# Four forms per expert, w1/w3 in 4 KB runs, and H accumulated chunk by chunk

## The chip, the cores and the metric

The kernel runs on one core of one Trainium2 chip. The metric is device time in microseconds (us) of one execution. Three runs of the kernel before gave 1067.29, 1071.5 and 1073.5 us, a median of 1071.5. The engines are called by their short names in the profile: PE (TensorE's matmuls), PEld (its weight loads), DVE (VectorE), ACT (ScalarE), POOL (GpSimd) and SP (SyncE, which issues most DMAs). A "q" behind a name (PEq, PEldq) is that engine's sequencer: it waits, branches or reads a count while the engine itself may go on with what is queued.

## The reference, cut to what matters

One layer of a hybrid attention / gating block over 1024 tokens of width 1024, followed by a mixture of experts. The change lies in the mixture alone. Every token picks one of four groups and two of its four experts; 16 experts, 512 hidden columns each:

```python
for e in range(N_EXPERTS):                                # 16
    hid = jax.nn.silu(t @ w1[e]) * (t @ w3[e])            # (1024, 512)
    out = out + gate[:, e:e + 1] * (hid @ w2[e])          # gate is zero but for two experts of a token
x = x + g_f * out
```

All arrays are float32. w1 and w3 are (16, 1024, 512), w2 is (16, 512, 1024): 6 MB of weights for an expert.

## The kernel before, in words

Before the mixture (up to about 606 us) come the modulation, the input projection, attention, gating, the output projection and the router. The router writes, for each expert, a list of its tokens, and leaves their numbers in `cnt`. From line 1536 on, the experts run one after the other in an order written out by hand: each engine executes its instructions in the order of the code.

**Tiles.** An expert takes its tokens in tiles of up to 128. `gather` (L1332) fetches the rows of a tile from `hfD` by an indirect DMA on POOL. `x_split` (L1338) transposes them on PE, eight pieces of 128 columns, and splits each into a high part (ACT) and a low part (DVE), so that a product in full float32 is made of three matmuls (`mm3`, L85: high x high, high x low, low x high). A tile of 64 tokens or fewer can go in the half form (`half_x`, `half_h`, `half_y`): the high part in the first 64 columns of the stationary operand, the low part in the other 64, so that two matmuls do in place of three and the two halves of the result are summed afterwards (`half_sum`, an ACT copy and a DVE addition). The first tile of an expert always goes in the full form, a second or third one by its count.

**Products.** H is computed in two halves f of its columns. A half (`h_mm`, L1350) takes 256 columns of w1 and 256 of w3 side by side: 8 x 3 matmuls of 512 columns. Then comes silu on ACT, a product on DVE, and `h_T` (L1362) transposes the 128 x 256 result in two pieces and splits it again. Y (`y_mm`) is 4 x 2 x 3 = 24 matmuls. So a full tile has 72 matmuls, a half one 48. `y_out` scales by the gate and adds the rows to `out` by an indirect DMA on POOL.

**Weights.** An expert's weights come in six chunks of 1 MB (`w_chunk`, L919): chunks 0 and 1 hold w1 and w3 of the first column half, 2 and 3 of the second, 4 and 5 hold w2. Chunks 0 to 3 read rows of 256 columns, 1 KB in one run; w2's runs have 4 KB. Seven raw buffers receive them; `e_conv` (L928) splits them into high parts (ACT, L941) and low parts (DVE or POOL, L946), 12 halves of 128 x 1024 for an expert, into six slots. A slot can be refilled when the expert before has finished with the chunk of the same number. A raw buffer that is free again starts the load of the chunk seven further on, from SP.

**Control flow.** `count(e)` (L1460) reads a count into a register on every engine, and `tc.If` becomes a branch on every engine. Bodies stand in the program in the order of the code; a body that isn't taken is jumped over. An expert e > 0 has an If for its second x (L1564, with `second`, L1470, choosing the form), one for the next expert's second gather (`gather_more`, L1466) and one for its second tile (`more1`, L1528: two bodies, 76 and 52 matmuls and transposes). Between them stand the first tile's parts and the conversions, written once. Expert 0's first `h_mm` is written right behind the reading of its count, outside every If.

Of the kernel before, what the change touches and what calls it, by code (L numbers as in the profile page):

```python
# [21 lines left out]
P = 128  # L22
# [17 lines left out]
def hybrid_layer_kernel(ctx, tc, a, out):  # L40
# [878 lines left out]
    def w_chunk(e, c, r, eng):  # L919
        if c < 4:  # L920
            for i, w in enumerate(("w1", "w3")):
                eng.dma_start(r.rearrange("p (k n) -> p k n", k=4)[:, :, i * 256:(i + 1) * 256],
                                  a[w][e, (c % 2) * 512:(c % 2) * 512 + 512, (c // 2) * 256:(c // 2) * 256 + 256].rearrange("(k p) n -> p k n", p=P))
        else:
            eng.dma_start(r.rearrange("p (k n) -> p k n", k=2),
                              a["w2"][e, (c - 4) * 256:(c - 4) * 256 + 256, :].rearrange("(k p) n -> p k n", p=P))

    def e_conv(g, i, eng=None):  # L928
        if g >= CH:
            return  # L930
        e_hi(g, i)
        if eng is None:
            eng = nc.gpsimd if g == 7 or i == 1 and (g == 6 or g >= 2 * 6 and g % 6 in (0, 5)) else nc.vector
        e_lo(g, i, eng)

    def e_hi(g, i):
        sl = slice(i * 1024, (i + 1) * 1024)
        if g == 7:
            nc.vector.tensor_copy(chi[g % NS][:, sl], raw[slot_of(g)][:, sl])
        else:  # L940
            nc.scalar.activation(chi[g % NS][:, sl], raw[slot_of(g)][:, sl], AF.Copy)  # L941

    def e_lo(g, i, eng):
        sl = slice(i * 1024, (i + 1) * 1024)
# [362 lines left out]
    def wk(e, c, k):  # L1307
        g = 6 * e + c
        n = 512 if c < 4 else 1024
        return chi[g % NS][:, k * n:(k + 1) * n], clo[g % NS][:, k * n:(k + 1) * n]  # L1310
# [9 lines left out]
    def bank4(j):  # L1320
        return bank(j, pst).rearrange("p (a n) -> p a n", a=4)
# [5 lines left out]
    hA = ep.tile([P, 256], F32, name="hA")  # L1327
    hB = ep.tile([P, 256], F32, name="hB")
# [9 lines left out]
    def x_split(j):  # L1338
        xg = (sc_f, xgi, xg2)[min(j, 2)]
        hi, lo = (xTi, xT0)[min(j, 1)]  # L1340
        for q in range(2):
            tr = bank4(j)
# [7 lines left out]
    def h_mm(e, j, f, hook=None):  # L1350
        hi, lo = (xTi, xT0)[min(j, 1)]
        po = bank(j, psh)
        for k in range(KD):
            wh, wl = wk(e, 2 * f + k // 4, k % 4)
            mm3(po, hi[:, k, :], lo[:, k, :], wh, wl, k == 0, k == KD - 1)
            if hook is not None and k == hook[0]:
                hook[1]()
        h = (hA, hB)[min(j, 1)]
        nc.scalar.activation(h, po[:, 0:256], AF.Silu)
        nc.vector.tensor_tensor(h, h, po[:, 256:512], op=ALU.mult)  # L1360

    def h_T(j, f):  # L1362
        hi, lo = hTs[min(j, 1)]
        h = (hA, hB)[min(j, 1)]
        tr = bank4(j)
        for i in range(2):
            nc.tensor.transpose(tr[:, i, :], h[:, i * P:(i + 1) * P], ident)  # L1367
        sl = slice(f * 2, f * 2 + 2)
        nc.scalar.activation(hi[:, sl, :], tr[:, 0:2, :], AF.Copy)
        nc.vector.tensor_tensor(lo[:, sl, :], tr[:, 0:2, :], hi[:, sl, :].bitcast(F32), op=ALU.subtract)  # L1370

    def y_mm(e, j, k0, k1):
        hi, lo = hTs[min(j, 1)]
        if k0 == 0:
            yss[j] = [bank(1, psy) for _ in range(2)]
        for k in range(k0, k1):
            wh, wl = wk(e, 4 + k // 2, k % 2)
            for i in range(2):
                sl = slice(i * 512, (i + 1) * 512)
                mm3(yss[j][i], hi[:, k, :], lo[:, k, :], wh[:, sl], wl[:, sl], k == 0, k == 3)  # L1380

    def y_out(e, j):
# [20 lines left out]
    def half_x(j):  # L1403
        xg = (xgi, xg2)[j - 1]
        for q in range(2):
            tr = bank4(1)
            for i in range(4):
                k = q * 4 + i
                nc.tensor.transpose(tr[:, i, 0:HP], xg[0:HP, k * P:(k + 1) * P], ident[0:HP, 0:HP])
            half_split(xT0[0][:, q * 4:q * 4 + 4, :], tr)  # L1410

    def half_h(e, j, f, hook=None):
        po = bank(1, psy)
        for k in range(KD):
            wh, wl = wk(e, 2 * f + k // 4, k % 4)
            nc.tensor.matmul(po, xT0[0][:, k, :], wh, start=k == 0, stop=False)
            nc.tensor.matmul(po, xT0[0][:, k, :], wl, start=False, stop=k == KD - 1)
            if hook is not None and k == hook[0]:
                hook[1]()
        s = xg2[0:HP, f * 512:(f + 1) * 512]  # L1420
        half_sum(s, po)
        h = hB[0:HP, :]
        nc.scalar.activation(h, s[:, 0:256], AF.Silu)
        nc.vector.tensor_tensor(h, h, s[:, 256:512], op=ALU.mult)

    def half_hT(f):
        tr = bank4(1)
        for i in range(2):
            nc.tensor.transpose(tr[:, i, 0:HP], hB[0:HP, i * P:(i + 1) * P], ident[0:HP, 0:HP])
        half_split(hTs[1][0][:, f * 2:f * 2 + 2, :], tr[:, 0:2, :])  # L1430

    def half_y(e, j, k0, k1):
        hs = hTs[1][0]
        if k0 == 0:
            yss[j] = [bank(1, psy) for _ in range(2)]
        for k in range(k0, k1):
            wh, wl = wk(e, 4 + k // 2, k % 2)
            for i in range(2):
                sl = slice(i * 512, (i + 1) * 512)
                nc.tensor.matmul(yss[j][i], hs[:, k, :], wh[:, sl], start=k == 0, stop=False)  # L1440
                nc.tensor.matmul(yss[j][i], hs[:, k, :], wl[:, sl], start=False, stop=k == 3)
# [12 lines left out]
    def conv2(g):  # L1454
        for i in range(2):
            e_conv(g, i)
# [13 lines left out]
    def second(e, j, one, other):  # L1470
        with tc.If(cr[e] > P * j + HP) as c:
            one()
        with c.Else():
            other()

    def x_more(e, j):
        second(e, j, lambda: x_split(j), lambda: half_x(j))

    def full(e, j):
        h_mm(e, j, 1, (2, lambda: h_T(j, 0)))  # L1480
        y_mm(e, j, 0, 1)
        h_T(j, 1)
        y_mm(e, j, 1, 4)
        y_out(e, j)

    def half(e, j):
        half_h(e, j, 1, (6, lambda: half_hT(0)))
        half_y(e, j, 0, 2)
        half_hT(1)
        half_y(e, j, 2, 4)  # L1490
        half_out(e, j)

    def more(e, j):
        def one():
# [4 lines left out]
            h_mm(e, j, 0)  # L1499
            full(e, j)  # L1500
# [3 lines left out]
        def other():  # L1504
            half_x(j)
            half_h(e, j, 0)
            half(e, j)
# [9 lines left out]
    def more1(e):  # L1517
        def one():
            if e == E - 1:
                with tc.If(cr[e] > P * 2):  # L1520
                    gather(e, 2)
            h_mm(e, 1, 0)
            full(e, 1)

        def other():
            half_h(e, 1, 0)
            half(e, 1)
        with tc.If(cr[e] > P):  # L1528
            second(e, 1, one, other)
# [159 lines left out]
```

## Time and profile before

| | |
|---|---|
| median of three runs | 1071.5 us |
| the profiled execution's own time | 1073.15 us |
| its span, first to last instruction | 1071.3 us |
| PE busy | 1004.6 us, 94% |
| PEld busy | 816.6 us, 76% |
| DVE busy | 735.4 us, 69% |
| ACT busy | 536.3 us, 50% |
| POOL busy | 381.6 us, 36% |
| moved by DMA | 255.26 MB, 238 GB/s on average |

Matmuls are pipelined, and their ends are modelled: one of 512 columns is shown as 0.39 us long while they start 0.23 us apart. A busy PE therefore says that matmuls follow each other without a gap, not that it runs at its peak; the distance between starts is the better measure. The granted clock is shown as a share of full speed. Idle time is put down to the engine that ended it; "PEq" there means that PE's own sequencer came late.

### The profile page before, as it was taken

How to read it: one execution, taken by the hardware profiler on the slowest of the kernel's cores; microseconds unless marked ns; L12 is line 12 of the kernel's file. 1: busy time of each engine (PE TensorE's matmuls, PEld its weight loads, DVE VectorE, ACT ScalarE, POOL GpSimd, SP SyncE). 2: the span in 40 equal slices, each digit the busy share in tenths (PEclk: the TensorE clock that was granted, in tenths of full speed). 3: DMA queues.
4: the chain of work that ended last, by engine and by line, in shares of the span. 5: the costliest groups of instructions: out<-in, count | busy, mean ns of one | idle time of the engine just before them, and what ended most of it. 6: DMA issues, size and time to landing. Idle time of an engine off the chain costs nothing. (4 is left out here: it accounts for less than half of the span.)

```text
span 1071.3 us, 15841 instructions
## 1 busy us (share of the span) xinstructions
PE 1004.6 (94%) x5161; PEld 816.6 (76%) x5161; DVE 735.4 (69%) x1478; ACT 536.3 (50%) x1024; POOL 381.6 (36%) x311
## 2 busy tenths in 40 slices
PE   9999899999999999999999888999998999999992
PEld 4688787876888989988888766777776888787771
DVE  2677658874627989967776858688888654765821
ACT  4643125243527989854322437476676543554611
POOL 1130321232302565641223554435645423243510
PEclk9999999999999999999999999999999999999997
DMA  9793605876757797959342698799999996886431
GB/s 325 271 316 134 200 1 177 287 237 243 252 210 263 253 352 265 322 182 324 122 149 80 202 299 287 247 332 353 346 360 353 343 294 201 292 257 194 131 60 16
DMA packets 138118, 255.26 MB, mean 238 GB/s; under 512 B 10310, under 2 KB 86726, under 8 KB 137994
## 3 DMA queue, kind: packets, MB, share of 16 engines
q1 hardware_dynamic: 122876, 201.57, 55.7%
q0 software_dynamic: 15120, 52.19, 16.1%
q8 instruction: 60, 0.98, 0.4%
q14 instruction: 62, 0.51, 0.2%
HBM read 210.45 MB, written 43.29 MB: 237 GB/s over the span
## 5 line engine op out<-in xcount | busy, mean ns | idle before, releaser
L946 DVE TENSOR_TENSOR clo<-raw,chi 128x1024 fp32r<-128x1024 f32 x140 | 174.2, 1291 | 18.8 <-ACT chi L941 17.7
L941 ACT ACTIVATE chi<-raw 128x1024 fp32r<-128x1024 f32 x166 | 162.6, 1049 | 1.5 <-DMA raw<-in_w 1.3
L86 PE MATMUL po<-whi,hhi 128*128 128x512 f32 x352 | 146.0, 415 | 0.0
L87 PE MATMUL po<-wlo,hhi 128*128 128x512 f32 x352 | 139.6, 397 | 0.0
L88 PE MATMUL po<-whi,hlo 128*128 128x512 f32 x352 | 139.3, 396 | 0.0
L1388 POOL DMA_INDIRECT out<-xb,lt x20 | 58.0, 2899 | 152.0 <-DVE xb L1387 152.0
L86 PE MATMUL b<-chi,yhi 128*128 128x512 f32 x256 | 104.7, 409 | 7.0 <-PEq L1528 4.1
L88 PE MATMUL b<-chi,ylo 128*128 128x512 f32 x256 | 101.7, 397 | 2.0 <-DVE ylo L1348 1.6
L87 PE MATMUL b<-clo,yhi 128*128 128x512 f32 x256 | 101.3, 396 | 0.0
L83 POOL TENSOR_TENSOR ss<-ss,nhalf 128x1 f32<-128x1 f32 (+1 forms) x36 | 46.0, 1276 | 144.2 <-DVE ss L82 144.0
L946 POOL TENSOR_TENSOR clo<-raw,chi 128x1024 fp32r<-128x1024 f32 x26 | 75.2, 2899 | 52.1 <-ACT chi L941 27.8
L86 PEld LDWEIGHTS po<-whi,hhi 128*128 128x128 f32 x352 | 66.7, 189 | 16.6 <-issue 2.6
L87 PEld LDWEIGHTS po<-wlo,hhi 128*128 128x128 f32 x352 | 66.8, 190 | 16.0 <-issue 2.4
L88 PEld LDWEIGHTS po<-whi,hlo 128*128 128x128 f32 x352 | 66.7, 189 | 15.9 <-DVE hlo L218 0.3
L86 PEld LDWEIGHTS b<-chi,yhi 128*128 128x128 f32 x256 | 48.4, 189 | 23.4 <-issue 8.4
L86 PE MATMUL yb<-chi,hhi 128*128 128x512 f32 x160 | 65.7, 411 | 0.0
L88 PE MATMUL yb<-chi,hlo 128*128 128x512 f32 x160 | 62.8, 393 | 0.0
L87 PE MATMUL yb<-clo,hhi 128*128 128x512 f32 x160 | 62.6, 391 | 0.0
L88 PEld LDWEIGHTS b<-chi,ylo 128*128 128x128 f32 x256 | 48.5, 190 | 14.1 <-DVE ylo L1348 2.1
L770 DVE TENSOR_TENSOR PT<-tr,PT 128x384 fp32r<-128x384 f32 (+1 forms) x128 | 56.4, 483 | 3.3 <-ACT PT L764 3.2
L87 PEld LDWEIGHTS b<-clo,yhi 128*128 128x128 f32 x256 | 48.5, 189 | 9.6
L572 DVE CUSTOM_DVE_ANT_0 S<-S,bt 128x640 f32<-128x640 f32 x64 | 52.7, 824 | 4.2 <-DMA bt<-in_btab 3.9
(316 smaller groups left out, 2343.7 us busy)
## 6 DMA issues: line engine op xcount, KB each, us to landing
raw<-in_w SPq DMA_DIRECT2D x104, 512.0 KB, 8.2
raw<-in_w SPq DMA_DIRECT2D x27, 1024.0 KB, 9.4
wraw<-in_w_ada SPq DMA_DIRECT2D x32, 512.0 KB, 5.1
v<-vD SPq DMA_DIRECT2D x16, 768.0 KB, 6.3
bt<-in_btab SPq DMA_DIRECT2D x32, 384.0 KB, 6.8
wraw<-in_w_in SPq DMA_DIRECT2D x20, 512.0 KB, 5.4
acc<-in_w SPq DMA_DIRECT2D x18, 512.0 KB, 7.4
wada<-in_w_ada SPq DMA_DIRECT2D x16, 512.0 KB, 6.6
```

Source lines behind the costliest of these rows:

```text
L83: nc.gpsimd.tensor_tensor(r, r, nhalf[:, :n], op=ALU.pow)
L86: nc.tensor.matmul(po, xh, wh, start=first, stop=False)
L87: nc.tensor.matmul(po, xh, wl, start=False, stop=False)
L88: nc.tensor.matmul(po, xl, wh, start=False, stop=last)
L572: nc.vector.tensor_tensor_reduce(sv, sv, btl[t, h // 2][:, h % 2 * 384:h % 2 * 384 + LK], op0=ALU.add, op1=ALU.max, scale=1.0, scalar=-3e3 ...
L770: nc.vector.tensor_tensor(lo, tr, hi.bitcast(F32), op=ALU.subtract)
L941: nc.scalar.activation(chi[g % NS][:, sl], raw[slot_of(g)][:, sl], AF.Copy)
L946: eng.tensor_tensor(lo[:, sl], r[:, sl], hi[:, sl].bitcast(F32), op=ALU.subtract)
L1388: nc.gpsimd.indirect_dma_start(out=out[:, :], out_offset=bass.IndirectOffsetOnAxis(ap=lt[:, e, j, 0:1], axis=0), in_=y, in_offset=None, co ...
```

## The change

Five things change together.

1. An expert's whole body is written four times (`expert`): one full tile, one half tile, two full tiles, a full and a half tile. Two nested If pick one by the count (expert 0 has three bodies). So a first tile of 64 tokens or fewer goes in the half form too. The x of the next expert gets its form inside the body (`next_x`).
2. Chunks 0 to 3 hold 256 rows of w1 and of w3 each, all 512 columns. Partition p takes eight rows in succession, p*8 to p*8+7, and a chunk two of them: one run of 4 KB per partition and matrix. To match, x is transposed by every eighth column (`cols`, and the first gather's `x_part`).
3. With each chunk that is there, both column halves of H advance (`h_part`), so two accumulators are open at a time.
4. A half of a chunk that is converted is now one of its two rows k, a view of 2 x 512 elements with a gap, and the third chunk's second half goes to POOL too.
5. `h_T`, `next_x` and the conversions (`fill`) stand at new places in the order; all transposes use the same two PSUM buffers, with one exception.

The diff, cut to its core:

```diff
     def w_chunk(e, c, r, eng):
         if c < 4:
             for i, w in enumerate(("w1", "w3")):
-                eng.dma_start(r.rearrange("p (k n) -> p k n", k=4)[:, :, i * 256:(i + 1) * 256],
-                                  a[w][e, (c % 2) * 512:(c % 2) * 512 + 512, (c // 2) * 256:(c // 2) * 256 + 256].rearrange("(k p) n -> p k n", p=P))
+                eng.dma_start(r[:, i * 1024:(i + 1) * 1024],
+                              a[w][e].rearrange("(p k) n -> p (k n)", k=KD)[:, c * 1024:(c + 1) * 1024])
...
-            eng = nc.gpsimd if g == 7 or i == 1 and (g == 6 or g >= 2 * 6 and g % 6 in (0, 5)) else nc.vector
+            eng = nc.gpsimd if g == 7 or i == 1 and (g == 6 or g >= 2 * 6 and g % 6 in (0, 2, 5)) else nc.vector
...
+    def part(w, g, i):
+        if g % 6 < 4:
+            return w.rearrange("p (m k n) -> p m k n", m=2, k=2)[:, :, i, :]
+        return w[:, i * 1024:(i + 1) * 1024]
...
     def e_lo(g, i, eng):
-        sl = slice(i * 1024, (i + 1) * 1024)
-        r, hi, lo = raw[slot_of(g)], chi[g % NS], clo[g % NS]
-        eng.tensor_tensor(lo[:, sl], r[:, sl], hi[:, sl].bitcast(F32), op=ALU.subtract)
+        r, hi, lo = part(raw[slot_of(g)], g, i), part(chi[g % NS], g, i), part(clo[g % NS], g, i)
+        eng.tensor_tensor(lo, r, hi.bitcast(F32), op=ALU.subtract)
...
-            nc.tensor.matmul(xg[k // 4][:, k % 4, :], src[:, k * P:(k + 1) * P], w, start=first and k % 4 == 0, stop=last and k % 4 == 3)
+            nc.tensor.matmul(xg[k // 4][:, k % 4, :], src.rearrange("p (n k) -> p k n", k=KD)[:, k, :], w, start=first and k % 4 == 0, stop=last and k % 4 == 3)
...
+    def w13(e, f, k):
+        g = 6 * e + k // 2
+        return [w[g % NS].rearrange("p (m k n) -> p m k n", m=2, k=2)[:, :, k % 2, f * 256:(f + 1) * 256] for w in (chi, clo)]
...
+    def cols(x, k):
+        return x.rearrange("p (n k) -> p k n", k=KD)[:, k, :]
...
-                nc.tensor.transpose(tr[:, i, :], xg[:, k * P:(k + 1) * P], ident)
+                nc.tensor.transpose(tr[:, i, :], cols(xg, k), ident)
...
+    def h_part(e, j, half, f, chunks):
         hi, lo = (xTi, xT0)[min(j, 1)]
+        for k in range(2 * chunks[0], 2 * chunks[-1] + 2):
+            if k == 0:
+                pos[j, f] = bank(j, psh)
+            po = pos[j, f]
+            wh, wl = w13(e, f, k)
+            if half:
+                nc.tensor.matmul(po, hi[:, k, :], wh, start=k == 0, stop=False)
+                nc.tensor.matmul(po, hi[:, k, :], wl, start=False, stop=k == KD - 1)
+            else:
+                mm3(po, hi[:, k, :], lo[:, k, :], wh, wl, k == 0, k == KD - 1)
+        if chunks[-1] == 3:
+            h = h_buf(j, half, f)
+            if half:
+                s = xg2[0:HP, f * 512:(f + 1) * 512]
+                half_sum(s, po)
+            else:
+                s = po
+            nc.scalar.activation(h, s[:, 0:256], AF.Silu)
...
+    def alone(e, j, half):
+        for c in range(3):
+            for f in range(2):
+                h_part(e, j, half, f, [c])
+        h_part(e, j, half, 0, [3])
+        h_T(j, half, 0)
+        h_part(e, j, half, 1, [3])
+        y_mm(e, j, half, 0)
+        h_T(j, half, 1)
+        for k in range(1, 4):
+            y_mm(e, j, half, k)
+        y_out(e, j, half)
...
+    def expert(e, n1, n2):
+        g0 = 6 * e
+        h1, h2 = n1 < P, n2 < P
+        def next_x():
+            if e + 1 < E:
+                with tc.If(cr[e + 1] > HP) as c:
+                    x_split(0)
+                with c.Else():
+                    half_x(0)
+            if e + 2 < E:
+                gather(e + 2, 0)
+        def second_x():
+            if n2 == P:
+                x_split(1)
+            else:
+                half_x(1)
+        halves = [(g0 + 4 + i // 2, i % 2) for i in range(12)]
+        def fill(n):
+            for _ in range(n):
+                e_conv(*halves.pop(0))
+        def chunk(j, half, c):
+            for f in range(2):
+                h_part(e, j, half, f, [c])
+        if not n2:
+            fill(2)
+            chunk(0, h1, 0)
+            gather_more(e + 1)
+            fill(3)
+            chunk(0, h1, 1)
+            fill(3)
+            chunk(0, h1, 2)
+            chunk(0, h1, 3)
+            h_T(0, h1, 0, bank(1, psy))
+            next_x()
+            y_mm(e, 0, h1, 0)
+            fill(1)
+            h_T(0, h1, 1)
+            y_mm(e, 0, h1, 1)
+            fill(3)
+            y_mm(e, 0, h1, 2)
+            y_mm(e, 0, h1, 3)
+            y_out(e, 0, h1)
+        elif e:
+            second_x()
+            for c in range(3):
+                fill(2)
+                chunk(0, h1, c)
+                if c == 0:
+                    gather_more(e + 1)
+                chunk(1, h2, c)
+            h_part(e, 0, h1, 0, [3])
+            h_part(e, 1, h2, 0, [3])
+            h_T(0, h1, 0)
+            h_part(e, 0, h1, 1, [3])
+            if not h2:
+                h_T(1, h2, 0)
+            h_part(e, 1, h2, 1, [3])
+            fill(1)
+            h_T(0, h1, 1)
+            if h2:
+                h_T(1, h2, 0)
+            y_mm(e, 0, h1, 0)
+            y_mm(e, 0, h1, 1)
+            fill(1)
+            h_T(1, h2, 1)
+            y_mm(e, 0, h1, 2)
+            y_mm(e, 0, h1, 3)
+            y_out(e, 0, h1)
+            fill(1)
+            y_mm(e, 1, h2, 0)
+            y_mm(e, 1, h2, 1)
+            next_x()
+            fill(1)
+            y_mm(e, 1, h2, 2)
+            y_mm(e, 1, h2, 3)
+            y_out(e, 1, h2)
+            fill(2)
+        else:
+            for c in range(3):
+                chunk(0, h1, c)
+            fill(2)
+            chunk(0, h1, 3)
+            fill(2)
+            second_x()
+            gather_more(1)
+            h_T(0, h1, 0)
+            for c in range(3):
+                chunk(1, h2, c)
+                if c == 0:
+                    h_T(0, h1, 1)
+                fill(2)
+            h_part(e, 1, h2, 0, [3])
+            if not h2:
+                h_T(1, h2, 0)
+            h_part(e, 1, h2, 1, [3])
+            if h2:
+                h_T(1, h2, 0)
+            y_mm(e, 0, h1, 0)
+            y_mm(e, 0, h1, 1)
+            h_T(1, h2, 1)
+            y_mm(e, 0, h1, 2)
+            y_mm(e, 0, h1, 3)
+            y_out(e, 0, h1)
+            fill(2)
+            next_x()
+            for k in range(4):
+                y_mm(e, 1, h2, k)
+            y_out(e, 1, h2)
...
+            count(e + 1)
+        with tc.If(cr[e] < P + 1) as one:
+            if e:
+                with tc.If(cr[e] > HP) as c:
+                    expert(e, P, 0)
+                with c.Else():
+                    expert(e, HP, 0)
+            else:
+                expert(e, P, 0)
+        with one.Else():
+            if e == E - 1:
+                with tc.If(cr[e] > P * 2):
+                    gather(e, 2)
+            with tc.If(cr[e] > P + HP) as c:
+                expert(e, P, P)
+            with c.Else():
+                expert(e, P, HP)
+    count(E)
```

`y_mm`, `h_T` and `y_out` get the argument `half` and do what `half_y`, `half_hT` and `half_out` did.

## Rows read from the trace of the kernel before

**Rows 1.** Timeline of PE in an expert with one tile: start, length, instruction.

```profile
740.38 0.47 PE L86 MATMUL b<-chi,yhi 128*128 128x512 f32 x1
...
751.95 0.39 PE L88 MATMUL b<-chi,ylo 128*128 128x512 f32 x1
752.18 1.03 PE L1345 MATMUL b<-ident,gf 128*128 128x128 f32 x8
...
755.43 0.44 PE L1367 MATMUL b<-ident,hA 128*128 128x128 f32 x2 [0.82 <-DVE ylo L1348]
```

**Rows 2.** Windows: busy us (instructions) of PE, PEld, DVE, ACT, POOL; clock, DMA share, GB/s.

```profile
300.00:400.00 100.00, 94.89 (x631) 86.92 (x629) 72.72 (x216) 67.60 (x188) 36.93 (x40) 0.98 0.75 263
...
740.30:760.10 19.80, 18.68 (x84) 14.46 (x84) 17.01 (x19) 13.78 (x20) 10.64 (x4) 1.00 1.07 353
```

**Rows 3.** Waits of PE and of SP, 606 to 1060 us: total us, times, longest.

```profile
PE yb L1440 <- DVE hhi L1401: 6.4, 5, 3.5
...
PE b L86 <- PEq L1528: 4.1, 2, 2.5
PE yb L1429 <- DVE hB L1424: 2.0, 5, 0.7
...
SPq L922 <- DVE clo L946: 125.5, 38, 13.7
```

**Rows 4.** Groups by line, 606 to 1060 us: the outputs of full and half tiles.

```profile
L1388 POOL DMA_INDIRECT out<-xb,lt x20 | 58.0, 2899 | 152.0 <-DVE xb L1387 152.0
...
L1451 POOL DMA_INDIRECT out<-xb,lt x4 | 5.8, 1447 | 42.0 <-DVE xb L1450 42.0
```

**Rows 5.** Groups by line, 606 to 1060 us: the sum of a half tile on DVE.

```profile
L1397 DVE TENSOR_TENSOR yb<-yb 64x512 f32<-64x512 f32 x16 | 10.8, 676 | 19.5 <-ACT yb L1396 19.5
```

**Rows 6.** Timeline of PE at the start of expert 0.

```profile
606.28 0.48 PE L86 MATMUL b<-chi,yhi 128*128 128x512 f32 x1
```

**Rows 7.** PE's sequencer by source line: ns (least/median/most), start us. Whole run, then windows.

```profile
L1528 PEldq COMPARE_BRANCH  x15: 65/325/6158, 649.3 to 1004.9; - x15
...
L1528 PEldq COMPARE_BRANCH  x1: 5514/5514/5514, 702.2 to 702.2; - x1
...
L1528 PEldq COMPARE_BRANCH  x1: 1683/1683/1683, 801.5 to 801.5; - x1
...
L1528 PEldq COMPARE_BRANCH  x1: 6158/6158/6158, 821.7 to 821.7; - x1
...
L1510 PEldq COMPARE_BRANCH  x1: 3347/3347/3347, 1050.7 to 1050.7; - x1
...
L1591 PEldq COMPARE_BRANCH  x1: 4742/4742/4742, 1054.1 to 1054.1; - x1
...
L1462 PEldq TENSOR_LOAD <-cnt x1: 489/489/489, 608.0 to 608.0; - x1
...
L1462 PEldq TENSOR_LOAD <-cnt x1: 304/304/304, 737.1 to 737.1; - x1
```

**Rows 8.** DMA queue q8, 300 to 400 and 740.3 to 760.1 us: packets, MB, share.

```profile
q8 instruction: 5, 0.08, 0.3%
...
q8 instruction: 2, 0.03, 0.7%
```

**Rows 9.** Timeline of PE behind the two longest branches at L1528.

```profile
707.85 0.47 PE L86 MATMUL b<-chi,yhi 128*128 128x512 f32 x1 [1.61 <-PEq L1528]
...
828.03 0.57 PE L86 MATMUL b<-chi,yhi 128*128 128x512 f32 x1 [2.47 <-PEq L1528]
```

**Rows 10.** Windows of 3.4 us behind them, columns as in rows 2.

```profile
707.80:711.20 3.40, 3.35 (x16) 2.78 (x17) 3.34 (x3) 3.23 (x5) 0.66 (x1) 1.00 1.02 316
...
827.90:831.30 3.40, 3.27 (x8) 2.63 (x9) 2.58 (x3) 1.90 (x3) 1.42 (x1) 0.55 1.12 307
```

**Rows 11.** PE's weight loads in `x_part`: timeline, then the group of the line.

```profile
604.37 1.75 PEld L1233 LDWEIGHTS xg<-sel,yb 128*128 128x128 f32 x15 [0.81 <-issue]
...
L1233 PEld LDWEIGHTS xg<-sel,yb 128*128 128x128 f32 x16 | 1.9, 191 | 0.8 <-issue 0.8
```

More of the change, by code (lines that the diff above doesn't have):

```diff
@@ L1318, in bank, with bank4 @@
         return first.tile([P, 512], F32, tag="b", name="b")
-    def bank4(j):
-        return bank(j, pst).rearrange("p (a n) -> p a n", a=4)
+    def bank4():
+        return bank(0, pst).rearrange("p (a n) -> p a n", a=4)
     xgi, xTi = y0, yT[0]
@@ L1325, in hybrid_layer_kernel @@
     xg2 = yb
-    hA = ep.tile([P, 256], F32, name="hA")
-    hB = ep.tile([P, 256], F32, name="hB")
+    hs = [ep.tile([P, 256], F32, name=f"h{i}") for i in range(3)]
     hTs = [[ep.tile([P, 4, P], F32R, name=f"{n}{j}") for n in ("hhi", "hlo")] for j in range(2)]
@@ L1348, in x_split @@
             nc.vector.tensor_tensor(lo[:, sl, :], tr, hi[:, sl, :].bitcast(F32), op=ALU.subtract)
-    def h_mm(e, j, f, hook=None):
+    pos = {}
+    def h_part(e, j, half, f, chunks):
         hi, lo = (xTi, xT0)[min(j, 1)]
[L1352 to L1360, printed above, removed]
@@ L1366, in h_T @@
         for i in range(2):
-            nc.tensor.transpose(tr[:, i, :], h[:, i * P:(i + 1) * P], ident)
+            nc.tensor.transpose(tr[:, i, 0:n], h[:, i * P:(i + 1) * P], ident[0:n, 0:n])
         sl = slice(f * 2, f * 2 + 2)
[L1369 to L1374, printed above, removed]
-            yss[j] = [bank(1, psy) for _ in range(2)]
[L1376 to L1379, printed above, removed]
+        if half:
+            half_split(hi[:, sl, :], tr[:, 0:2, :])
+        else:
+            nc.scalar.activation(hi[:, sl, :], tr[:, 0:2, :], AF.Copy)
+            nc.vector.tensor_tensor(lo[:, sl, :], tr[:, 0:2, :], hi[:, sl, :].bitcast(F32), op=ALU.subtract)
@@ new lines, in y_mm @@
+    def y_mm(e, j, half, k):
+        hi, lo = hTs[1 if half else min(j, 1)]
+        if k == 0:
+            yss[j] = [bank(1, psy) for _ in range(2)]
+        wh, wl = wk(e, 4 + k // 2, k % 2)
+        for i in range(2):
+            sl = slice(i * 512, (i + 1) * 512)
+            if half:
+                nc.tensor.matmul(yss[j][i], hi[:, k, :], wh[:, sl], start=k == 0, stop=False)
+                nc.tensor.matmul(yss[j][i], hi[:, k, :], wl[:, sl], start=False, stop=k == 3)
+            else:
@@ L1403, in half_x @@
     def half_x(j):
-        xg = (xgi, xg2)[j - 1]
+        xg = (sc_f, xgi, xg2)[j]
         for q in range(2):
-            tr = bank4(1)
+            tr = bank4()
             for i in range(4):
                 k = q * 4 + i
[L1409 to L1441, printed above, removed]
+                nc.tensor.transpose(tr[:, i, 0:HP], cols(xg[0:HP, :], k), ident[0:HP, 0:HP])
+            half_split((xTi, xT0)[min(j, 1)][0][:, q * 4:q * 4 + 4, :], tr)
     def half_out(e, j):
@@ L1452, in half_out, with y_out @@
                                      in_=y, in_offset=None, compute_op=ALU.add)
-    def conv2(g):
-        for i in range(2):
-            e_conv(g, i)
+    def y_out(e, j, half):
+        (half_out if half else full_out)(e, j)
     cr = {}
@@ L1467, in gather_more @@
                 gather(e, 1)
[L1470 to L1491, printed above, removed]
+    def alone(e, j, half):
[10 more added lines that the diff above has]
+        y_out(e, j, half)
     def more(e, j):
@@ L1498, in one @@
                     gather(e, j + 1)
-            h_mm(e, j, 0)
-            full(e, j)
+            alone(e, j, False)
             if j + 1 < T // P:
@@ L1505, in other @@
             half_x(j)
-            half_h(e, j, 0)
-            half(e, j)
+            alone(e, j, True)
         with tc.If(cr[e] > P * j):
@@ L1515, in more @@
                 one()
[L1517 to L1529, printed above, removed]
+    def expert(e, n1, n2):
[75 more added lines that the diff above has]
+            fill(2)
+        else:
+            for c in range(3):
[28 more added lines that the diff above has]
+            y_out(e, 1, h2)
```

73 lines of the change are left out of this document (17 added, 56 removed).

## The prediction

> **What bounds the kernel now.** I read the page first, then the waits of TensorE in the expert stage (606 to 1060 us), then single experts in order of time. One expert with one tile, from 740.3 to 760.1 us, holds 72 matmuls that start 0.23 us apart (751.95 to 752.18), 12 transposes of about 0.1 us (8 in 1.03) and one wait of 0.82 us before the transposes of H's second half [rows 1]. In those 19.80 us PE is busy 18.68, DVE 17.01, and the DMA share is 1.07 [rows 2]. So TensorE sets the pace; VectorE and DMA are close behind. The waits say the same: TensorE waits longest in the chain of a half tile (L1440, 6.4 us in 5 times; L1429, 2.0 in 5) and for its own sequencer at L1528 (4.1 in 2); no weight load is in the list. SyncE, for its part, waits for free buffers (125.5 us for DVE's conversions): the loads run ahead [rows 3].
>
> Which experts take which path: the reference's router on its inputs gives 163, 29, 162, 68, 94, 116, 109, 85, 59, 29, 193, 201, 146, 194, 124 and 276 tokens. The trace has 20 full and 4 half outputs [rows 4], which is what these counts give (16 first tiles, 4 full and 3 half second ones, one half third). In the new kernel experts 3 to 7 and 14 are alone and full, 1, 8 and 9 alone and half, 0, 2 and 12 full plus half, 10, 11, 13 and 15 full plus full.
>
> **The change part by part.** The sum is made against the profiled execution's own 1073.15 us (span 1071.3 and 1.85 around it); the median shown is 1071.5, 1.65 less.
>
> *Half form for three first tiles.* 48 matmuls in place of 72, so 3 x 24 x 0.232 = 16.7 us of TensorE less. A half tile's chain is longer: four of them waited 6.4 + 2.0 - 3.5 (one odd wait) = 4.9 us [rows 3], 1.2 each, and with some 0.2 to start again after each of four waits 2.0: +6. VectorE gets four sums of 0.68 [rows 5], 2.7, and loses one conversion, about 1.3, to GpSimd: 17.0 + 1.4 = 18.4 us per such expert, which binds only if TensorE needs less.
>
> *Both halves of H by chunks.* In the six full experts that are alone, H's first half is ready while the second half's last matmuls run: the 0.82 us wait and its restart, about 1.0, goes six times, -6. In the three experts with a half second tile I take -1 each for waits of the chain, -3 (bounds 0 and -2.2 each).
>
> *Expert 0.* Its matmuls start at 606.28 now [rows 6], before the count is read at 608.0 to 608.5 [rows 7]. After the change all of them stand inside the If: +2.9 with the second count. Its 3.5 us wait in the half tile's chain (the longest at L1440) [rows 3] should go with the interleaving: -3.5. Together -0.6.
>
> *Code that is skipped.* This decides. Each expert now is written out four times, and all five engines branch. Instruction code comes over q8 in packets of 16 KB (5 packets, 0.08 MB, from 300 to 400 us, where TensorE ran 631 matmuls [rows 2, 8]: one per 126, and so I take q8 for TensorE's). Skipped code is fetched like run code: 2 packets in the one expert at 740 us, where 84 ran [rows 8]. The old kernel skips the second tile's two bodies (76 + 52 = 128 matmuls, about one packet) at L1528, in the nine experts with one tile. Of the branches there, taken or not, the median is 0.33 us. Three are not like that: 5.51, 1.68 and 6.16 us [rows 7]. The skip past the rest of the third tile took 3.35 us, the one to the end 4.74 [rows 7]. I read: what is at hand is the packet in use and the next, the next once it has landed; a branch beyond that waits 3.35 (DMA quiet) to 6.16 us (share 1.07). TensorE has matmuls queued meanwhile: it reads the count at 737.1 while the next expert's first matmul starts at 740.38, so some 3.1 us are covered [rows 1, 7], and of the 5.51 and 6.16 us, 1.61 and 2.47 came through as idle time [rows 9].
>
> In the new kernel the bodies hold, in matmuls and transposes: alone full 92 (72 + 4 + both forms of the next x, 16), alone half 68, full plus full 176, full plus half 152. An alone full expert skips 68 + 328 at its end, three packets: never at hand. An alone half one skips 92 ahead and 328 behind. Full plus full skips 160 ahead and 152 behind, full plus half 160 and then 176. I count 13 skips that come out of running code (nine ends of experts 1, 3 to 9 and 14; around 10, 11, 12 and 13 four more) and 8 that follow another skip with no matmul between (0, 1 each at 8, 9, 10, 12 and 15, and two at expert 2). Price of one: bounds 3.35 and 6.16; I take 4.3, nearer to the quiet rows, because the pause itself lets the loads run dry and 4 KB runs take less of the DMA's time. The first kind shows 4.3 - 3.1 = 1.2 each, 15.6; the second all of it, 8 x 4.3 = 34.4. Together +50.
>
> [...]
>
> *Old stalls that go.* The two idle times at L1528 and the slow stretch behind one of them: (1.61 + 2.47, less 0.15 that a short branch costs) 3.8 + 1.7 = -5.5.
>
> *Clock.* [...] 8 matmuls ran in the one stretch and 16 in the other [rows 9, 10], so a slow one loses 7 to 8 matmuls, 1.7 us. I take four of them, +7 (bounds 0 and 13 stretches, 22).
>
> *4 KB runs for w1 and w3.* They shorten transfers that no TensorE wait names; nothing on the path, 0. Without that cover a load would show as a wait of the conversions on DMA.
>
> *Conversions.* Fourteen more halves go from VectorE to GpSimd. GpSimd is busy 10.64 of 19.80 us [rows 2]; one more conversion fits. The strided view keeps 1024 elements per instruction: 0, bounds -2 and +5.
>
> *x by every eighth column.* 216 weight loads of transposes (and of the first gather) now step 32 bytes. The trace has no such load. Nearest rows: loads of 0.19 us each still go at 0.117 (15 in 1.75 us) [rows 11], so somewhat longer loads cost nothing to speak of: +2. Upper bound, each load its whole 0.19 us longer: +41; a gain is excluded, since no load gets less to do.
>
> **Sum:** -16.7 + 6 - 6 - 3 - 0.6 + 50 - 5.5 + 7 + 2 = +33. 1073.15 + 33 = 1106; by the median 1104.
>
> **Rivals.**
> *The code is at hand (faster).* If branches find their target as six of nine do now, the 50 and the 7 fall away: -24. Then TensorE would need 48 x 0.232 + 1.2 + 2 = 14.4 us in a half expert, and VectorE's 18.4 sets experts 8 and 9, which gives back some 5: -19, 1052. It decides when skips cost under some 24 us in all, 1.1 each. For it: the median branch of 0.33 us [rows 7]. Against: nearly all the new skips are longer than one packet.
> *Nothing shows.* Skips at the quiet price with all of the first kind covered and no slow clock: 8 x 3.35 = 27 against gains of 24: 1075. For it: the skips of 3.35 us in quiet stretches. Against: most of the experts stage is not quiet.
> *The other engines' skips as well.* Their code too jumps, and it feeds TensorE: a pause in VectorE after its branch delays the next x and the conversions. VectorE has 2.8 us free per 19.8 [rows 2]. One pause of 3 us that shows in half the experts is +24: 1128. For it: five engines take each branch. Against: most pauses fall together.
> *Strided loads.* At 0.12 more per load, 216 x 0.12 = 26: 1128. [...]
>
> **How the numbers follow.** Forecast 0.48, with its own range 1084 (price 3.35) to 1130 (price 5.5); code at hand 0.20; nothing shows 0.07; other engines 0.15; strided loads 0.10. Faster 0.20, within 0.5% 0.07, slower 0.73; 0.5%, 5 us, is about what a measurement of this kernel can tell from no change. The range 1051 to 1133 leaves out part of the first rival and part of the last two.
>
> **What would show it.** Right: branches of PE's sequencer at the new If lines that last 3.3 to 6.2 us, about 20 of them; idle of PE put down to its own queue of some 50 us, most behind experts 2, 10, 12 and 15; more stretches at half clock; 72 fewer matmuls of 512 columns; the 0.82 us wait gone in experts 3 to 7; transposes of x still at 0.1 us. Wrong: these branches under 1 us, or PE's busy time short of its matmuls' while DVE or a DMA ends its waits.

## The result, and the profile after

The changed kernel takes 1185.2 us (median; 1180.84 to 1191.39) against 1071.8, a ratio of 1.107 [1.101, 1.113]: slower, as forecast, but by 113 us and not by 33, and above the stated range. The profiled execution has a span of 1181.3 us.

The page of the changed kernel, its first part (busy us, share of the span, instructions):

```profile
PE 1020.7 (86%) x5089; PEld 829.0 (70%) x5089; DVE 759.0 (64%) x1476; ACT 544.8 (46%) x1036; POOL 403.4 (34%) x325
```

There are 72 matmuls fewer (5161 before), as the counts said. All the loss is in the expert stage. The stage as one window, columns as in rows 2, first before and then after:

```profile
606.00:1053.00 447.00, 420.87 (x1917) 331.68 (x1916) 305.73 (x371) 240.36 (x343) 186.92 (x86) 0.99 0.84 266
```

```profile
606.00:1166.00 560.00, 436.51 (x1849) 343.56 (x1849) 328.69 (x363) 248.95 (x354) 209.30 (x100) 0.90 0.65 211
```

It is 113 us longer (both windows end with the stage's last matmul), and TensorE's idle time grew from 26 to 123 us (447 - 421, 560 - 437). Its mean clock fell from 0.99 to 0.90: matmuls that start late, mostly 0.43 us apart in place of 0.23, with no idle time between them, cost 30 us over PE's timeline, 5 before. VectorE is busy 23 us more, though 14 of its conversions in the stage moved to GpSimd (156 before, 142 after).

The waits of PE in the stage (total us, times, longest), which answer to [rows 3]:

```profile
PE b L1446 <- issue: 26.3, 2, 13.7
PE b L1373 <- DVE clo L951: 14.8, 2, 7.8
PE b L1356 <- issue: 14.3, 3, 6.5
PE b L1398 <- DVE yb L1385: 12.1, 3, 8.7
PE b L86 <- DVE clo L951: 11.8, 2, 7.6
PE yb L1398 <- DVE yb L1385: 11.3, 3, 6.6
PE b L86 <- DVE xb L1424: 10.4, 4, 3.7
PE yb L1398 <- DVE h L1385: 7.1, 3, 3.4
```

No row names PE's sequencer. The branches themselves do, PE's sequencer by line, then one window (count, ns least/median/most), which answer to [rows 7]:

```profile
L1643 PEldq COMPARE_BRANCH  x18: 68/4081/6591, 661.2 to 1102.8; - x18
...
L1641 PEldq COMPARE_BRANCH  x16: 73/81/5646, 610.9 to 1106.1; - x16
...
L1653 PEldq COMPARE_BRANCH  x11: 65/2339/7959, 611.2 to 1142.4; - x11
...
L1643 PEldq COMPARE_BRANCH  x1: 4297/4297/4297, 782.3 to 782.3; - x1
```

22 branches inside the experts last 2.3 to 8.0 us, 4.4 on average; two packets of code come over q8 while the one at 782.3 waits. PE's timeline, which answers to [rows 1, 9]:

```profile
701.12 1.12 PE L1446 MATMUL b<-ident,y 64*128 64x64 f32 x8 [13.67 <-issue]
...
787.59 0.47 PE L86 MATMUL b<-chi,yhi 128*128 128x512 f32 x1 [2.78 <-DVE xb L1424]
...
801.23 0.44 PE L1398 MATMUL yb<-ident,h 128*128 128x128 f32 x2 [2.34 <-DVE h L1385]
```

The pause before 787.59 is put down to VectorE, but it ends behind the branch of 4.30 us that began at 782.3. So add up idle times by place: those that end at or behind one of the 22 branches make 78 us, 4 before. The 13.67 us at 701.12 lie behind three such branches in a row at the head of expert 2. The pause at 801.23 is another matter: there H's product comes late from VectorE, with no branch near.

Windows of an expert with one full tile, and of 3.4 us behind a pause of 3.66 us, columns as in rows 2; they answer to [rows 2, 10]:

```profile
786.70:811.30 24.60, 18.58 (x84) 14.56 (x84) 21.20 (x19) 16.19 (x21) 11.09 (x5) 1.00 0.95 316
...
812.20:815.60 3.40, 3.40 (x10) 2.73 (x11) 2.81 (x3) 0.00 (x0) 1.99 (x1) 0.64 1.02 319
```

The same work takes 24.6 us in place of 19.8. VectorE is busy 21.2, with fewer conversions than the 17.0 of before held.

Weight loads by strided x (ns least/median/most), which answer to [rows 11]:

```profile
L1238 PEld LDWEIGHTS xg<-sel,yb x16: 312/336/338, 603.8 to 607.4; 128*128 128x128 f32 x16
```

They take 336 ns where the trace of before had 0.19 us for the same group [rows 11].

### The profile page after: what moved, and what is told of

Same layout as the page of the kernel before. It is cut to its first block, busy times and chain, and to the rows that moved or that the text cites. A ratio compares the mean times of both kernels' runs of the same rounds, so it can differ in the third digit from the quotient of the medians.

```text
span 1181.3 us, 15660 instructions
## 1 busy us (share of the span) xinstructions
PE 1020.7 (86%) x5089; PEld 829.0 (70%) x5089; DVE 759.0 (64%) x1476; ACT 544.8 (46%) x1036; POOL 403.4 (34%) x325
## 4 chain that ended last, share of the span: by engine, by line
PE 48%; DMA 17%; issue 14%; DVE 9%; POOL 4%; ACT 3%; another core or an unknown queue 3%; POOLq 0%; DVEq 0%; SPq 0%; ACTq 0%
PE po L86 5%; PE po L88 5%; PE po L87 5%; DMA raw<-in_w 4%; DMA out<-xb,lt 3%; PE OT L781 3%; POOL clo L951 3%; DVE clo L951 2%; PE tr L762 2%; PE yb L86 2%; PE yb L88 2%; PE yb L87 2%; PE pa L248 2%; PE b L86 2%
## 5 line engine op out<-in xcount | busy, mean ns | idle before, releaser
L951 DVE TENSOR_TENSOR clo<-raw,chi 128x1024 fp32r<-128x1024 f32 x128 | 191.4, 1532 | 39.0 <-ACT chi L947 33.8
L951 POOL TENSOR_TENSOR clo<-raw,chi 128x1024 fp32r<-128x1024 f32 x38 | 102.2, 2709 | 76.1 <-ACT chi L947 45.5
L86 PE MATMUL b<-chi,yhi 128*128 128x512 f32 x208 | 89.8, 432 | 23.5 <-DVE clo L951 11.8
L1425 POOL DMA_INDIRECT out<-xb,lt x17 | 35.3, 2074 | 163.5 <-DVE xb L1424 153.1
L87 PE MATMUL b<-clo,yhi 128*128 128x512 f32 x208 | 86.9, 418 | 0.0
L88 PE MATMUL b<-chi,ylo 128*128 128x512 f32 x208 | 86.8, 417 | 0.0
L1385 DVE TENSOR_TENSOR h<-h,b 128x256 f32<-128x256 f32 x26 | 10.5, 416 | 82.1 <-ACT h L1384 81.9
L86 PE MATMUL yb<-chi,hhi 128*128 128x512 f32 x136 | 57.3, 422 | 0.0
L86 PE MATMUL po<-woh,yhi 128*128 128x512 f32 (+1 forms) x136 | 54.7, 402 | 0.0
L87 PE MATMUL yb<-clo,hhi 128*128 128x512 f32 x136 | 54.4, 400 | 0.0
```

The lines of the kernel that those rows point to most:

```text
L86: nc.tensor.matmul(po, xh, wh, start=first, stop=False)
L87: nc.tensor.matmul(po, xh, wl, start=False, stop=False)
L88: nc.tensor.matmul(po, xl, wh, start=False, stop=last)
L951: eng.tensor_tensor(lo, r, hi.bitcast(F32), op=ALU.subtract)
L1425: nc.gpsimd.indirect_dma_start(out=out[:, :], out_offset=bass.IndirectOffsetOnAxis(ap=lt[:, e, j, 0:1], axis=0), in_=y, in_offset=None, co ...
```

## The experiments

Theory A: the skipped code is what costs. Theory B: the new order, with conversions spread over VectorE and GpSimd, costs as much by itself. From e5 on B became theory C: VectorE and GpSimd hold each other up. Ratios are to the kernel before, run on the same chip beside each; the runs lie on four chips, where its medians are 1071.3 to 1073.1 us.

### e1: no branches

```diff
-        with tc.If(cr[e] < P + 1) as one:
...
+        n = N[e]
+        expert(e, P if n > HP else HP, 0 if n <= P else HP if n <= P + HP else P)
```

`N` holds this input's counts; `next_x` and `gather_more` choose by it too.

> Each expert keeps the one body that this input's counts ask for, chosen when the program is written; the choice by count inside the experts is left out, all else is as in the changed kernel. Theory A (skipped code is what costs): the 78 us that TensorE stands idle behind branches and nearly all of the 25 us more at half clock go, so 1181 - 78 - 25 = about 1078, 1070 to 1092. Theory B (the new order of conversions, gathers and chains costs as much by itself, and would be late anyway): what stood behind branches turns up as waits for VectorE, 1110 to 1150.

1130.1 us, 1.054 [1.049, 1.059]. The time lies in theory B's range, but neither theory had the whole: the skips are worth 55 us, and 58 stay that have nothing to do with branches. Matmuls at half rate still cost 27 us, against 30 with the skips. One expert of this run, PE, then VectorE, then GpSimd:

```profile
825.82 0.69 PE L1398 MATMUL yb<-ident,h 128*128 128x128 f32 x2 [4.42 <-DVE h L1385]
```

```profile
813.48 9.68 DVE L951 TENSOR_TENSOR clo<-raw,chi 128x1024 fp32r<-128x1024 f32 x4
823.09 2.35 DVE L951 TENSOR_TENSOR clo<-acc,chi 128x1024 fp32r<-128x1024 f32 x2
825.36 0.74 DVE L1385 TENSOR_TENSOR h<-h,b 128x256 f32<-128x256 f32 x2
```

```profile
815.61 5.33 POOL L951 TENSOR_TENSOR clo<-raw,chi 128x1024 fp32r<-128x1024 f32 x2
```

Two conversions take VectorE 2.35 us when it is by itself, and four take 9.68 while GpSimd does two of its own. The product that makes H stands behind all six in VectorE's order, and TensorE waits 4.42 us for it, and some of the matmuls behind the wait start 0.43 us apart. This repeats in each expert with one full tile that follows another (24.2 to 24.8 us each). Over the stage, VectorE's 142 conversions take 64 us more than 1.22 us each in this run and 46 more in the changed kernel; in the kernel before, its 156 took 11 more.

The trace of before had the sign of it, in rows that the prediction passed over:

```profile
749.88 1.22 DVE L946 TENSOR_TENSOR clo<-acc,chi 128x1024 fp32r<-128x1024 f32 x1
...
751.96 2.48 DVE L946 TENSOR_TENSOR clo<-raw,chi 128x1024 fp32r<-128x1024 f32 x1 [0.21 <-ACT chi L941]
```

```profile
750.50 2.85 POOL L946 TENSOR_TENSOR clo<-acc,chi 128x1024 fp32r<-128x1024 f32 x1 [3.28 <-ACTq L1528]
753.32 3.37 POOL L946 TENSOR_TENSOR clo<-raw,chi 128x1024 fp32r<-128x1024 f32 x1
```

The same conversion takes 1.22 us when GpSimd is idle at its start, and 2.48 when it starts 1.4 us before GpSimd's ends (1.4 + 1.1). It waits, and does not share: eight conversions of VectorE in that stage start while GpSimd converts, and each ends 1.08 to 1.09 us after GpSimd's, whether 1.4 or 2.3 us of that one were left.

### e2 and e3: a skip by itself, in the kernel before

```diff
+    def pad(e):
+        with tc.If(cr[e] > T - 1):
+            b = bank(0, pst)
+            for i in range(328):
+                nc.tensor.matmul(b, xTi[0][:, i % KD, :], chi[0][:, 0:512], start=True, stop=True)
...
+        pad(e)
```

e3 has 40 in place of 328.

> The kernel before, with a body of 328 matmuls that is never taken (2.6 packets of code for TensorE, next to nothing for the others) at the head of each of 15 experts. Theory A: each skip takes about 4.3 us, of which TensorE's queue covers 2.1 to 3.1, and 1 us goes by until the first matmul: 15 x 2.2 to 3.2 = 33 to 48, and half clock behind some of them 10 to 20: 1115 to 1140. Theory B (a skip alone is hidden by queued matmuls in this kernel): under 1085.

> As the last, but the body that is never taken has 40 matmuls, a third of a packet. Theory A (length decides: what is at hand is the packet in use and the next): most branches at 0.3 us, 1072 to 1082. Rival: a branch that is taken costs the same whatever it skips: as much as with 328 matmuls.

e2: 1161.1 us, 1.084 [1.079, 1.089], 90 us for 15 skips, more than either expected. e3: 1075.6, 1.005 [1.002, 1.007]. Length decides. The branch of the skip and, behind it, the old short one at L1528 in e2, then the skip in e3:

```profile
L1532 PEldq COMPARE_BRANCH  x15: 3790/5503/6373, 640.1 to 1087.4; - x15
...
L1528 PEldq COMPARE_BRANCH  x15: 65/1937/5885, 648.8 to 1094.5; - x15
```

```profile
L1532 PEldq COMPARE_BRANCH  x15: 202/208/417, 639.7 to 1004.0; - x15
```

A long skip also slows the next short one: at L1528 nine of the 15 branches skip 128 matmuls and transposes, and the median of the 15 rises from 0.33 to 1.94 us. Little of that reaches TensorE, whose idle time there is 4.8 us, 4.1 before. The 6 us of a skip here are its own wait and the clock behind it: 56 us of idle time end at the long skips, one of them with another branch of 6 us close behind, and matmuls at half rate cost 31 us in place of 5 (mean granted clock 0.952, before 0.984).

### e4: everything but the four bodies

```diff
+    def more1(e):
+        second(e, lambda: alone(e, 1, False), lambda: alone(e, 1, True))
...
+            chunk(0)
+            gather_more(e + 1)
+            fill(2)
+            more1(e)
+            fill(1)
+            chunk(1)
```

> The control flow of before (first tile always full and written once, short Ifs around a second tile), with everything else of the change: 4 KB runs, x by every eighth column, both halves of H by chunks, the new engines for the conversions, the order of the new body for one full tile. Theory A: only code was dear, so the 0.82 us waits go and nothing is added: 1058 to 1072. Theory B: these parts cost by themselves: 1085 to 1100.

1138.5 us, 1.061 [1.056, 1.066]: theory B, and more than its 1085 to 1100. PE's first wait in the stage:

```profile
PE yb L1398 <- DVE h L1385: 36.0, 11, 8.1
```

It is e1's wait again, without the skips of whole bodies.

### e5 and e6: GpSimd converts no more, and a new order

```diff
-            eng = nc.gpsimd if g == 7 or i == 1 and (g == 6 or g >= 2 * 6 and g % 6 in (0, 2, 5)) else nc.vector
+            eng = nc.gpsimd if g == 7 or i == 1 and g == 6 else nc.vector
```

That is e5, on e1. e6 adds, in the bodies for one tile:

```diff
-            fill(3)
+            fill(2)
             chunk(0, h1, 1)
-            fill(3)
+            fill(2)
...
             y_mm(e, 0, h1, 1)
-            fill(3)
+            fill(5)
```

> The kernel with fixed bodies of the first run, and GpSimd converts nothing from expert 2 on: all twelve halves of an expert go to VectorE. Theory C (a conversion on GpSimd holds VectorE's up: two of 1.22 us took 3.4 each beside two on GpSimd, and the product that makes H, behind them, came 4.4 us late in each expert): VectorE then has 8 halves and the output's 1.4 ahead of that product, 11.2 us where some 9 are there, so 2 late in place of 4.4: 1095 to 1115. Rival D (VectorE has too much to do, and its mean rose because of that): three more halves of 1.22 make every expert 2 to 4 us longer, 1145 to 1170.

> As the last, and of the twelve halves six in place of eight stand ahead of H's product in the bodies for one tile. Theory C: 6 x 1.22 + 1.4 = 8.7 us fit into the 9 that are there, the wait goes, and with it most of the time at half clock: 1060 to 1085. Rival D: as late as in the last, no gain from the order.

e5: 1098.4 us, 1.024 [1.020, 1.028], 32 less than e1 although VectorE does three halves more per expert: theory C, and rival D falls. e6: 1089.8, 1.015 [1.011, 1.020], 8.5 less again, but not the 1060 to 1085 expected.

### e7: e4 with both edits

The edits of e5 and e6 on e4.

> The kernel with the control flow of before and the rest of the change, with both edits: all halves on VectorE, and six of twelve ahead of H's product. Theory C: its period of 23.8 us for an expert with one tile falls to 20 to 20.5, and the experts with two tiles keep their 2 us: 1138 - 9 x 3.5 - 20 = 1075 to 1100. Rival D, or a cost of the 4 KB runs or of the strided x: above 1115.

1104.4 us, 1.029 [1.025, 1.033]: 34 less than e4, and above what was expected. Between two readings of the count, an expert with one tile takes 19.4 to 19.6 us, less than the 19.8 of before, but one with two full tiles 38.8 in place of 35.9: there TensorE waits 1.4 us for the split of the second x and 1.0 for the product of its H, and the kernel before waits for neither.

### e8: the third half on GpSimd, in the kernel before

```diff
-            eng = nc.gpsimd if g == 7 or i == 1 and (g == 6 or g >= 2 * 6 and g % 6 in (0, 5)) else nc.vector
+            eng = nc.gpsimd if g == 7 or i == 1 and (g == 6 or g >= 2 * 6 and g % 6 in (0, 2, 5)) else nc.vector
```

> The kernel before with one edit, the third chunk's second half on GpSimd too. Theory C: VectorE saves 1.22 and loses up to 2 us beside GpSimd in each expert from 2 on, if the two meet: 1071 to 1086. If GpSimd's work were free for VectorE: 1066 to 1072.

1067.8 us, 0.997 [0.994, 0.999], below theory C's range. The edit is harmless in the old order, though the two engines do meet: GpSimd's third half runs while the output is scaled, and 14 of VectorE's conversions take 2.1 us, but the product of H that comes next still waits 1.15 us for ScalarE. So it is not the number of GpSimd's conversions that costs, but their meeting VectorE's where H's product stands close behind; here it had that time to spare.

### e9: e5's edit with the branches left in

The one line of e5, on the changed kernel.

> The changed kernel, branches and all, with one edit: GpSimd converts nothing from expert 2 on. If the two costs add up, skips and conversions, it gains what the same edit gained with fixed bodies, 32 us: about 1153. If the pauses of the skips give VectorE time to catch up, it gains less: 1160 to 1178.

1188.8 us, 1.107 [1.101, 1.114]: no gain at all, where both expectations had one. A new wait takes the place. GpSimd, then VectorE, then PE:

```profile
787.61 10.26 POOL L1425 DMA_INDIRECT out<-xb,lt  x1 [6.99 <-DVE xb L1424]
```

```profile
787.25 2.35 DVE L951 TENSOR_TENSOR clo<-raw,chi 128x1024 fp32r<-128x1024 f32 x2
789.51 2.36 DVE L951 TENSOR_TENSOR clo<-acc,chi 128x1024 fp32r<-128x1024 f32 x2
791.78 4.63 DVE L951 TENSOR_TENSOR clo<-raw,chi 128x1024 fp32r<-128x1024 f32 x4
```

```profile
806.36 0.45 PE L1356 MATMUL b<-ident,gf 128*128 128x128 f32 x1 [7.66 <-DMA out<-xb,lt]
```

The indirect DMA that mostly took GpSimd 1.5 to 2.4 us in the changed kernel takes 10.26 while VectorE converts eight halves in a row, and ends 1.5 us behind them (797.87, 796.41). The rows of the output land late, and the next x's transposes wait for them: 7.7, 8.4 and 8.6 us in three experts. The transposes read other rows than these; the program with branches makes them wait for that DMA too. The fixed bodies of e5 have the same 10.3 us, but no such wait.

### e10: no half form for a first tile

```diff
-    N = [163, 29, 162, 68, 94, 116, 109, 85, 59, 29, 193, 201, 146, 194, 124, 276]
+    N = [163, 128, 162, 68, 94, 116, 109, 85, 128, 128, 193, 201, 146, 194, 124, 276]
```

> Fixed bodies, all on VectorE, six halves ahead of H's product, and experts 1, 8 and 9 in the full form (128 rows each, most of them empty): 72 matmuls more, 16.7 us of TensorE. If the half form is paced by VectorE and its chain, as the waits of 5.3 and 7.0 us in experts 8 and 9 say, the full form is as fast or faster: 1076 to 1088. If the half form saves what its matmuls say: 1100 to 1108.

1080.55 us, 1.007 [1.004, 1.010], 9 less than e6 with 72 matmuls more. Expert 8 in e6 (half), then the same in e10 (full), columns as in rows 2:

```profile
813.20:834.00 20.80, 14.99 (x62) 11.43 (x61) 18.17 (x23) 14.12 (x21) 8.81 (x2) 0.84 1.03 383
```

```profile
804.70:823.40 18.70, 18.21 (x85) 14.60 (x84) 17.79 (x21) 13.97 (x19) 8.81 (x2) 1.00 1.03 386
```

The half form leaves VectorE 18.2 us of work, as forecast, so nothing can be won below that; and its sums wait behind conversions, which costs TensorE a pause of 5.3 us; its mean clock over the expert is 0.84. VectorE, then PE, in e6 (L1434 is the sum):

```profile
817.63 6.89 DVE L951 TENSOR_TENSOR clo<-raw,chi 128x1024 fp32r<-128x1024 f32 x6
824.44 0.67 DVE L1434 TENSOR_TENSOR yb<-yb,b 64x512 f32<-64x512 f32 x1
```

```profile
826.07 0.47 PE L1398 MATMUL yb<-ident,yb 64*128 64x64 f32 x2 [5.31 <-DVE yb L1385]
```

### e11, e12 and e15: the 0.82 us wait of the kernel before

```diff
-    def h_T(j, f):
+    def h_T(j, f, spare=False):
...
-        tr = bank4(j)
+        tr = bank4(j or spare)
...
-        h_T(0, 1)
+        h_T(0, 1, True)
         conv2(g0 + 7)
```

This and e8's line are e15; e11 has `bank4(j or f)` alone, in expert 0 too, and e12 is e11 with e8's line.

> The kernel before with one edit: the transposes of H's second half take a buffer of the four for Y and of second tiles, in place of one of the two that the next x has just filled. If the 0.82 us wait is for that buffer and not for H: it goes in 7 to 9 experts, 1071.7 - 6 to 9 = 1062 to 1066. If it is for H: no change.

> The last, and the third chunk's second half on GpSimd too, which alone gave 0.3%. If the two add up: 1058 to 1063. If VectorE, once TensorE waits less, has no time left for GpSimd's turns: 1064 to 1070.

> The kernel before, the third chunk's second half on GpSimd, and the spare buffer for H's second transposes from expert 1 on, not in expert 0, where it held Y up by 2.3 us. Periods of 19.2 in place of 19.8 in eight experts, and nothing lost at the start: 1061 to 1066, faster than both. If the gain is lost again in the experts with two tiles: 1067 to 1071.

e11: 1072.5 us, 1.001 [0.997, 1.004], not the 1062 to 1066 expected. e12: 1069.4, 0.998 [0.996, 1.001]. The wait goes (19.2 to 19.4 us between counts in place of 19.8, seven times), so it was for the buffer; but in expert 0 the borrowed one holds Y up by 2.33 us. e15: 1064.4 us, 0.992 [0.989, 0.994], faster than both kernels.

### e13 and e14: what is left in e10

```diff
-        return x.rearrange("p (n k) -> p k n", k=KD)[:, k, :]
+        return x[:, k * P:(k + 1) * P]
```

That is e13, with the same in `x_part`; e14:

```diff
-            eng = nc.gpsimd if g == 7 or i == 1 and g == 6 else nc.vector
+            eng = nc.vector
...
-        if g == 7:
-            nc.vector.tensor_copy(hi, r)
-        else:
-            nc.scalar.activation(hi, r, AF.Copy)
+        nc.scalar.activation(hi, r, AF.Copy)
```

> The kernel with fixed bodies, all full, all conversions on VectorE, and x taken again in blocks of 128 adjacent columns, where the changed kernel takes every eighth (so columns of x and rows of w1, w3 no longer belong together: only the time is of use). If the loads of strided x cost what they show (334 ns in place of 192 in the first gather, 48 of them one behind the other, 6 us; some 2 more in the experts): 1080.5 - 8 = 1070 to 1075. If they are hidden: 1079 to 1083.

> The same kernel with the strided x, and the conversions of expert 1's first two chunks, which run inside expert 0, leave GpSimd as well (high parts to ScalarE, low parts to VectorE). If the 8.75 us that TensorE waits in expert 0 come from VectorE and GpSimd holding each other up: 4 to 6 less, 1074 to 1077. If they come from the chain of the half tile itself: 1079 to 1083.

e13: 1076.8 us, 1.005 [1.002, 1.007]; e14: 1077.4, 1.005 [1.003, 1.006]. Each is some 3 us below e10, about the width of the intervals, so the times alone don't settle either; their rows do. The loads of e13, then PE's wait in expert 0 in e10 and in e14:

```profile
L1238 PEld LDWEIGHTS xg<-sel,yb x16: 186/192/192, 601.9 to 603.5; 128*128 128x128 f32 x16
```

```profile
644.36 0.45 PE L1398 MATMUL b<-ident,yb 64*128 64x64 f32 x2 [8.75 <-DVE yb L1385]
```

```profile
643.43 0.45 PE L1395 MATMUL b<-ident,yb 64*128 64x64 f32 x2 [4.43 <-DVE yb L1382]
```

### e16: the same 15 skips in e10

> The kernel with fixed bodies, all full, all conversions on VectorE, and in front of 15 experts a body of 328 matmuls that is never taken. If a skip costs here what it cost in the kernel before (90 us for 15, 6 each): 1080.5 + 75 to 95 = 1155 to 1175. If the waits that are left swallow part of the pauses, as with the changed kernel's 55 us for some 22: 1115 to 1140.

1123.4 us, 1.050 [1.046, 1.054]: 43 us for 15 skips, 2.9 each. The branches:

```profile
L1627 PEldq COMPARE_BRANCH  x15: 3332/5097/5931, 653.7 to 1047.9; - x15
```

They come at two levels, 3.3 to 3.7 us (7) and 5.1 to 5.9 (8). With no other skip close behind, and matmuls queued ahead, that is the price of one.

## Why the prediction was wrong

The sign was right and so was the mechanism of the skips, but the sum was 81 us short: some 40 of them are the conversions, 20 the half form, and 20 the rest, half of that in expert 0. By the order in which the parts were taken out:

| term | forecast | measured | by |
|---|---|---|---|
| skipped code, with its half clock | +57 | +55 | e1 |
| conversions: engines and order | 0 | +40 (32 + 8.5) | e5, e6 |
| half form for three first tiles | -10.7 | +9 | e10 |
| strided x | +2 | about +4 | e13 |
| the rest (H by chunks, expert 0, old stalls, 4 KB runs) | -15 | +5 | what stays |
| sum | +33 | +113 | |

The parts overlap, so another order gives other shares: with all conversions on VectorE the skips are worth 90 us (e9 against e5), in part because the next x then waits for the late DMA (25 us in three waits). No run takes out the 4 KB runs alone (forecast 0); they are in the rest. The traces show that q1 needed a little less of the DMA engines' time for the same 90.45 MB: 58.3% of 454 us before (606 to 1060), 45.8% of 560 after (606 to 1166), 265 and 256 us.

*Skips.* Right in number and price: 22 branches of 4.4 us on average for 21 at 4.3. How they show was not: 78 us of idle time in place of 50, since TensorE, at 782.3 for one, had 2.5 us queued and not 3.1, and needed 1.0 us from the branch's end to its first matmul. That e1's 55 comes close to 57 is in part luck: without the skips other waits grow, from 45 us of idle time to 75, and nearly all of the half clock stays.

*Conversions: the step that failed.* "0, bounds -2 and +5." The step asked whether GpSimd had time for one more, and did not ask what GpSimd's time does to VectorE. e1, e5 and e6 price it at 40 us. e8 shows that the number of GpSimd's halves is not the fault by itself; it is that eight of twelve halves now stand ahead of H's product, GpSimd's beside VectorE's, so that VectorE waits there and TensorE behind it.

*Half form.* The 18.4 us of VectorE were worked out (18.17 measured in e6), then used for a rival alone, while the sum took TensorE's 16.7. The sums' place behind conversions was missed: waits of 5.3 and 7.0 us in place of 1.2.

*Both halves of H by chunks.* The wait of 0.82 us does go, but not for the reason forecast. It was not for H: its row names `ylo`, the next x's low part [rows 1], and e11 removes it with another buffer alone, which is worth 0.6 us an expert. That one with a full tile takes 18.7 us in e10 where it took 19.8, about the 1.0 that was forecast, is in part luck: e10 has no branches between experts, and with the short ones of before (e7) it is 19.4 to 19.6. In the changed kernel the gain is buried under 2.3 us for H's product.

*Expert 0.* Forecast -0.6. From its first H matmul to expert 1's it takes 10 us more in e10 than before (49.2 and 39.2 us), with no branch: a wait of 8.75 us, 8.74 in the changed kernel too, behind conversions that VectorE and GpSimd share, of which e14 takes 4.3. The other part, in the new order of expert 0, was not tried.

*Clock.* Forecast +7 for four stretches; 25 us more than before. Matmuls at half rate, 0.43 us apart (at 862.9 to 867.0 with a granted clock of 0.50), stand behind 17 of the 21 pauses over 2 us (before: 2 of 2; e1: 14 of 14, one of them with transposes, and without a branch between experts). So it is a cost of most long waits, not of skips.

*Strided x.* The rival's price, 0.12 us a load, for which no row stood, is what the first gather shows (0.24 us between starts and 0.12 before [rows 11], 48 loads, 6 us; one load takes 336 ns and took 192), but the transposes of the next x hardly slow down, 1.09 us for eight where it was 1.03 [rows 1].

No rival reached 1185. "The other engines' skips as well" had VectorE late, but for another cause: not its branches, but its conversions, held up by GpSimd's in the way of H.

## What to carry to other kernels

Before work moves between VectorE and GpSimd, look in the trace for one instruction with two durations (1.22 and 2.48 us here): that difference, times the meetings, is the price, and it counts most ahead of an instruction that TensorE waits for (4.42 us in an expert of e1). A form that saves TensorE time is worth only what the engine that then sets the pace allows (VectorE's 18.2 us in expert 8 of e6), so work out that engine's load in the sum itself. A body that is written out several times costs about 3 (e16) to 6 us (e2) for each long skip, so a variant must save more than that in every iteration.

## What the runs showed of the hardware

- How long a skip's branch takes depends on what is skipped and what went before: 0.2 us for 40 matmuls (e3), 3.3 to 3.7 or 5.1 to 5.9 for 328 (e16), and at L1528, where nine of 15 branches skip 128, 1.94 in the median with a skip of 328 ahead of each (e2), 0.33 without (before).
- A VectorE conversion that starts while GpSimd converts ends 1.08 to 1.09 us after GpSimd's, eight times of eight in the kernel before: it waits for all that is left.
- VectorE holds GpSimd up too: an indirect DMA that took 2.3 us in the median (the changed kernel, 17 times) took 10.26 beside eight conversions in a row (e9).
- The idle time's releaser can be innocent: the pauses behind branches of 4 to 8 us carried the names of VectorE's instructions or "issue".
